# A hybrid encoder trunk on one core: quarters of the array in turn, logits of two heads in one step, and a bank shared between attention and state space

## The chip, the cores and the metric

The kernel runs on one core of a Trainium2 chip. The metric is the device time of one execution in microseconds. In the rows PE is TensorE's matmul, PEld its weight load, DVE is VectorE, ACT is ScalarE, POOL is GpSimd and SP is the queue that issues nearly all DMAs.

## The reference

Two layers work on one sequence of 256 tokens with 1024 features. All is float32.

```
h = rmsnorm(x, norm_g[l]);  proj = h @ w_in[l]            # 1024 -> 5120
xa, za, qb, kb, vb, zb, qc, kc, vc, zc = split(proj)      # ten parts of 512
ya = ssm_branch(xa, ...) * silu(za)        # 32 groups of 16 channels, 64 complex states, two directions
yb = na_branch(qb, kb, vb, rpb) * silu(zb) # 8 heads of 64, neighbourhood attention on a 4 x 64 grid
yc = dilated_branch(qc, kc, vc, t5) * silu(zc)  # 8 heads of 64, three dilated windows
x = x + concatenate([ya, yb, yc]) @ w_out[l]
```

A final rmsnorm follows. The state-space branch ends in a gated product with glu_w (512 x 512).

## The kernel before

Every step is a small Python generator. It yields the engine that it wants next, the buffer slots that it takes (`SLOTS` says how many of each there are) and the events that it waits for. A planner (`Flow`) holds a clock for each engine, adds an assumed cost for each instruction (`charge`), and always advances the step that can start first, less a patience and then by rank (`RANK`, `PATIENCE`). What comes out is one fixed order of instructions for each engine; on the chip every engine works its list off in that order.

The weights come in pieces of 512 KB (`raw`). A piece for a split product is rounded to a high part on ACT or DVE (`whi`, about 1 us) and its remainder is taken on DVE (`wlo`); then 24 matmuls use it (`mm3`, records `pj<-...`). Some pieces are used unsplit as plain float32. The step `products` runs through the pieces: 20 column blocks of w_in, then w_out and glu_w. All else stands between its matmuls in PE's list.

PSUM has eight banks, and the kernel takes all: `pj` 3, `sc` 1, `pp` 1, `po` 1, `sm` 2. The attention of a layer is 16 steps of `head` (two branches of 8 heads). A head takes `sc`, makes its logits in two matmuls with 64 rows of the array (even heads have their 64 features on partitions 0 to 63, odd ones on 64 to 127), adds the bias and takes the row maximum on DVE (tile `pt`), frees `sc`, takes exponentials on ACT, scales by the reciprocal sums, takes `pp` for four transposes, copies them to `ptt` on ACT, and after the odd head of two the products with v go to `po`. The buffers `pt`, `ptt` and `bias` have two slots each.

The state-space branch takes `sm` for all its steps. It works in 4 blocks of 8 groups, and 4 groups at a time each use 32 columns of the array (a quarter, `tile_position=(0, 32 * g4)`), so that each writes its own 32 partitions of one bank. The tiles are named after the steps: `psx` (`ssm_x`: inputs to states; it goes through the four quarters in its innermost loop already, and through whole-array transposes of the same name after that), then a scan on DVE, `psr` (`ssm_kernels`: with 16 matmuls of 128 columns and 16 of 16 columns a block), and `psy` (`ssm_y`: 24 matmuls of 128 columns a block). In `psr` and `psy` all matmuls of one quarter come before those of the next. From `psr` the kernel goes through ACT and DVE (`rs`) to DRAM and comes back as `toep`; from `psy` it goes through DRAM (`yd`) to `yT`, GELU and the gated product.

Every float32 matmul (operands not split) stands in the trace as two records.

Of the kernel before, what the change touches and what calls it, by code (L numbers as in the profile page):

```python
# [20 lines left out]
P = 128  # L21
# [4 lines left out]
HEADS = 8  # L26
HD = 64
GROUPS = 32
NST = 64
CH = 16  # L30
T = 8
# [22 lines left out]


SLOTS = dict(raw=3, whi=3, wlo=2, act=3, qkv=6, g4=8, wb=6, qrp=2, tm=3, toep=1, E=1, u=5, bias=2, t2k=2, pt=2, ptt=2,
            xa=1, sg=5, xt=1, hy=1, bd=1, bs=1, rs=1, yt=1, ys=3, tab=1, atn=1, pj=3, sc=1, pp=1, po=1, sm=2)

PLAIN = ((0, 1, 2, 3, 5, 8), (0, 1))

# [10 lines left out]
            gelu=(AF.Gelu_apprx_tanh, AF.Tanh))  # L71
# [8 lines left out]
            place=(0.4, 5.3), ssm_params=(7.3, 5.6), ssm_start_values=(7.6, 6.2), ssm_angles=1.5, normed=(2.8, 1.0),  # L80
            split_h=(0.2, 2.6), finish=(3.7, 3.1), put_out=0.7, high_parts=(4.6, 0.2), low_parts=(8.6, 8.2),
            low_by_dma=(1.5, 1.7), to_xa=(7.7, 1.9), to_u=(3.7, 8.8), to_qkv=(3.7, 5.7), to_gate=(8.0, 0.4),
            keep_x=(2.7, 8.1), head=(2.5, 0.5), gelu=(9.0, 0.2), to_mix=(5.2, 1.4), to_x=(7.4, 1.4), load_pieces=1.5,
            into_loads=(7.4, 6.4), into_powers=(0.1, 5.1), t5_rows=(1.9, 5.1), biases=(5.2, 7.9), reload_x=(1.3, 4.3),
            bias_glu=(8.7, 6.0), ssm_x=(3.8, 7.6), ssm_scan=(6.7, 3.1), ssm_kernels=(5.2, 4.9), ssm_y=(3.7, 3.6),
            ssm_tables=(2.1, 7.5), ssm_into=5.0, ssm_out=(0.8, 5.3), products=(5.2, 1.2))
# [9 lines left out]
            to_mix=(0.339, 0.3), reload_x=(-0.3, 0), bias_glu=0.1, place=(0.8, 0.195), split_h=(0.15, 0.249),  # L96
# [17 lines left out]
class Event:  # L114
    t, eng = None, None
# [24 lines left out]
def _count(x):  # L140
    n = 1
    for _, m in x.ap[1:]:
        n *= m
    return n
# [9 lines left out]
class Flow:  # L154
# [16 lines left out]
    def charge(self, eng, method, args, kw):  # L171
        out = args[0] if args else kw["out"]
        c = self.cur
        start = max(self.clock[eng], c.at, c.ready + (0.0 if c.last == eng else _latency(c.last, eng)))
        if method == "dma_start":
            spread = args[1].ap[0][1] < 64 and out.ap[0][1] == P
            self.clock[eng] = c.ready = start + (1.05 if eng == "G" else 0.65 if spread else 0.475)
            c.last = eng
            d = max(self.clock["DMA"], self.clock[eng] + 0.65)
            n = _count(out) * (out.ap[0][1] if out.ap[0][1] <= P else 1) * 4  # L180
            self.clock["DMA"] = d + max(n / 360e3, 0.06)
            c.pend = max(c.pend, self.clock["DMA"] + 0.85)
            return
        n = _count(out)
        if eng == "PE":
            if method == "transpose":
                cost = 0.109
            else:
                m, r = _count(kw["lhsT"]), kw["rhs"]
                passes = 1 if r.dtype == F32R else 4  # L190
                cost = max(_count(r) / 2400.0 * passes, 0.054) + (0.0025 if passes == 1 else 0.005)

                if m < 16:
                    pass
                elif m <= 32:
                    cost = (cost + 3 * 0.027) / 4
                elif m <= 64:
                    cost = (cost + 0.053) / 2
                else:
                    cost = max(cost, 0.107)  # L200
        elif eng == "V":
            one = method in ("tensor_scalar", "tensor_copy", "tensor_scalar_mul", "tensor_scalar_add", "memset")
            cost = 0.07 + n / (1920.0 if one else 960.0)
            if any(not isinstance(x, (float, int)) and x is not None and not isinstance(x, ALU) for x in args[2:3] if one):
                cost += 0.065
            if method == "reciprocal":
                cost = 0.06 + n * 0.0065
        elif eng == "A":
            cost = 0.1 + n * 0.00082 + (0.18 if "accum_out" in kw else 0.05 if "bias" in kw else 0.0)
            if method == "mul" and not isinstance(args[2], float):  # L210
                cost += 0.09
            if method == "activation" and args[2] in HOME and args[2] not in SETS.get(self.table, ()):
                self.table = HOME[args[2]]
                cost += 1.28
        else:
            cost = 0.1 + n * 0.0023
        if eng != "G":
            start = max(start, c.pend)
        if eng == "PE":

            if start - self.clock[eng] > IDLE:
                self.cold = start + COLD
            if start < self.cold:
                cost *= 2
        c.ready = self.clock[eng] = start + cost
        c.last = eng
# [112 lines left out]
def trunk(ctx: ExitStack, tc: tile.TileContext, io):  # L339
    nc = tc.nc  # L340
    flow = Flow(tc)
    V, A, G, PE, SP = flow.V, flow.A, flow.G, flow.PE, flow.SP
# [9 lines left out]
    def bank(tag, name=None):  # L352
        return psum.tile([P, 512], F32, name=name or tag, tag=tag, bufs=SLOTS[tag])
# [19 lines left out]
    def mm(out, lhsT, rhs, start, stop):  # L373
        PE.matmul(out, lhsT=lhsT, rhs=rhs, start=start, stop=stop, skip_group_check=True)
# [36 lines left out]
    bd = one("bd", [2, GB, CH, 2])  # L411
# [490 lines left out]
    def ssm_kernels(L, b, tb, wcs):  # L902
        bb = tb.bb
        yield "A", "bd", "bs"
        bs = new("bs", [2, GB, CH, 2])
# [4 lines left out]
        for d in range(2):  # L910
            r = slice(d * NST, (d + 1) * NST)
# [3 lines left out]
        yield "PE", "sm"  # L915
        ps = bank("sm", "psr")
        n = (T + 1) * CH
        for h in range(2):
            for g4 in range(4):
                g = 4 * h + g4  # L920
                o = ps[32 * g4:32 * g4 + 32, h * n:(h + 1) * n]
                for ri in range(2):
                    PE.matmul(o[:, :T * CH], lhsT=bd[:, ri, g].rearrange("p c d -> p (c d)"),
                              rhs=wcs[h][:, ri, g4].rearrange("p t c -> p (t c)"),
                              start=(h == 0 and ri == 0), stop=ri == 1, skip_group_check=True,
                              tile_position=(0, 32 * g4))
                for ri in range(2):
                    PE.matmul(o[:, T * CH:], lhsT=bs[:, ri, g].rearrange("p c d -> p (c d)"),
                              rhs=tb.cc[:, ri, b * GB + g], start=False, stop=ri == 1,
                              skip_group_check=True, tile_position=(0, 32 * g4))  # L930
        flow.free("bd", "bs")
        yield "A", "rs"
        rs = new("rs", [2, T + 1, CH])
# [28 lines left out]
    def ssm_y(L, b, tb):  # L962
# [8 lines left out]
        wcs, u, toep = tb.wc[b], L.u[b], tb.toep[b]  # L971
        py = bank("sm", "psy")
        for h in range(2):
            for g4 in range(4):
                g = 4 * h + g4
                o = py[32 * g4:32 * g4 + 32, h * P:(h + 1) * P]
                PE.matmul(o, lhsT=u[:, g, :], rhs=toep[:, g, :], start=h == 0, stop=False,
                          skip_group_check=True, tile_position=(0, 32 * g4))
                for ri in range(2):
                    PE.matmul(o, lhsT=hy[:, ri, g, :], rhs=wcs[h][:, ri, g4].rearrange("p t c -> p (t c)"),  # L980
                              start=False, stop=ri == 1, skip_group_check=True, tile_position=(0, 32 * g4))
        flow.free("toep" if b < TOEP else "qkv", "g4", "g4", "u", "hy")
        tb.y_left -= 1
        if tb.y_left == 0:
# [81 lines left out]
    def near(t, qt):  # L1066
        return free(t, FAR * (1 - qt), [[GRID_W, 4], [1, NEAR]])

    def grid(t, qt):
        return free(t, S * qt, [[GRID_W, 4], [1, NEAR]])  # L1070

    def head(L, br, h):
        B = L.br[br]
        hp, hh = h // 2, h % 2
        r = slice(HD * hh, HD * hh + HD)
        yield "PE", "sc", B.q_ev[hp // 2], B.k_ev[hp // 2]
        sc = bank("sc").rearrange("p (q k) -> p q k", q=2)
        for qt in range(2):
            o, q, k = sc[:, qt, :], B.qkv[0].tile[r, hp, qt * P:(qt + 1) * P], B.qkv[1].tile[r, hp, :]
            if br == 0:  # L1080
                o, k = grid(sc, qt), near(k, qt)
            mm(o, q, k, qt == 0, True)
        B.sc_left -= 1
        if B.sc_left == 0:
            flow.free("qkv", "qkv")
            if br == 1:
                flow.set(L.sc_ev)
        bias = L.bias[br]
        nm, sm = one("nm", [2], bufs=4), one("sm", [2], bufs=4)
        if br == 0:  # L1090
# [19 lines left out]
        for qt, (p, _, _) in enumerate(parts):  # L1110
            eng = yield "A/V"
            scale(eng, p, p, sm[:, qt:qt + 1])
        yield "PE", "pp"
        pp = bank("pp").rearrange("p (k q) -> p k q", k=2)
        for qt in range(2):
            for kt in range(2):
                PE.transpose(pp[:, kt, qt * P:(qt + 1) * P], pt[:, qt, kt * P:(kt + 1) * P], ident)
        flow.free("pt")

        yield ("A", "ptt", "ptt") if hh == 0 else ("A", B.ptt_ev[h - 1])  # L1120
        ptt = B.ptt[h] = new("ptt", [2, S])
        A.copy(ptt, pp)
        flow.free("pp")
        flow.set(B.ptt_ev[h])
        if hh == 0:
            return
# [266 lines left out]
    def run_layer(L):  # L1393
# [3 lines left out]
        for kind, c, kgs in L.jobs:  # L1397
            if kind == "in":
# [31 lines left out]
                if c == 1:  # L1430
                    ssm_run(L, tbs[l])
                    flow.spawn(biases(L), l)
                    for br in range(2):
                        for h in range(HEADS):
                            flow.spawn(head(L, br, h), l)
                    flow.spawn(reload_x(L), l)
                    flow.spawn(bias_glu(L), l)
            elif kind == "glu":
# [233 lines left out]
```

## Time and profile before

| what | value |
|---|---|
| median of 3 runs | 517.58 us (512.52 to 519.69) |
| the profiled execution | 511.08 us, of which 509.3 us span |
| TensorE clock granted, mean of the span | 0.981 |
| busy: PE, PEld, DVE, ACT | 95%, 86%, 75%, 58% |
| chain that ended last | PE 67%, DMA 20%, DVE 6% |

The span runs from the first to the last instruction; 1.8 us lie around it. Busy shares are means over stages that differ, so the table by stage counts for more than this one. Layer 0 takes about the first 260 us, layer 1 the rest.

### The profile page before, as it was taken

What the parts mean: (1) busy time and instruction counts of PE and PEld (TensorE: products, weight loads), DVE (VectorE), ACT (ScalarE), POOL (GpSimd) and SP (SyncE); (2) the same over time, 40 slices, a digit from 0 to 9 for tenths busy, and PEclk for the clock granted to TensorE, in tenths of its full rate; (3) what the DMA queues carried; (4) which work ended last, traced back from release to release, by engine and by line L of the source; (5) the groups of instructions that cost most, each with busy time, mean ns of one, the idle gap of its engine ahead of it and who ended that gap; (6) DMA issues with size and microseconds to landing.
All of it is one profiled execution on the core that took longest, in us unless ns stands there. A gap on an engine that the chain in (4) does not pass through costs nothing.

```text
span 509.3 us, 10599 instructions
## 1 busy us (share of the span) xinstructions
PE 483.6 (95%) x4076; PEld 436.0 (86%) x4076; DVE 381.3 (75%) x745; ACT 297.0 (58%) x596; POOL 24.6 (5%) x45
## 2 busy tenths in 40 slices
PE   8887988999999999989999699999999999999995
PEld 7676786698888999989998599998989799999995
DVE  5966767988997895457879678889788994358533
ACT  6432366566587665455545436767676776587432
POOL 1000102110000000000000010222000000000000
PEclk9988999999999999999999889999999999999999
DMA  7987798865663779874767997877565585664512
GB/s 261 299 236 247 218 258 232 222 172 166 140 143 106 219 260 278 245 215 162 252 205 211 262 268 204 186 170 178 136 126 134 138 261 182 184 167 168 187 41 84
DMA packets 73331, 99.61 MB, mean 196 GB/s; under 512 B 26768, under 2 KB 48400, under 8 KB 73280
## 3 DMA queue, kind: packets, MB, share of 16 engines
q1 hardware_dynamic: 73136, 98.83, 70.1%
q8 instruction: 32, 0.52, 0.4%
q14 instruction: 19, 0.16, 0.1%
q10 hardware_dynamic: 144, 0.10, 0.1%
HBM read 93.19 MB, written 5.72 MB: 194 GB/s over the span
## 4 chain that ended last, share of the span: by engine, by line
PE 67%; DMA 20%; DVE 6%; SPq 2%; ACT 2%; issue 2%; POOL 0%; DVEq 0%; POOLq 0%; ACTq 0%
PE pj L135 45%; PE psr L135 6%; PE sc L135 5%; DMA raw<-w_in 4%; DMA wb<-b_c 3%; DMA u<-xad 3%; PE po L135 3%; PE pp L135 3%; PE psy L135 3%; SPq L135 2%; DVE wb L135 2%; PE psx L135 2%; DMA qd<-qbt 2%; DMA raw<-w_out 1%; DMA xad<-xa 1%
## 5 line engine op out<-in xcount | busy, mean ns | idle before, releaser
L135 DVE TENSOR_TENSOR wlo<-raw,whi 128x1024 fp32r<-128x1024 f32 x92 | 113.6, 1234 | 55.6 <-PE pj L135 28.6
L135 ACT CAST whi<-raw 128x1024 fp32r<-128x1024 f32 x91 | 95.0, 1048 | 67.3 <-DMA raw<-w_in 28.2
L135 PE MATMUL pj<-h0h,whi 128*128 128x256 f32 x192 | 58.3, 304 | 0.0
L135 PE MATMUL pj<-h1h,whi 128*128 128x256 f32 x192 | 56.3, 293 | 0.0
L135 PE MATMUL pj<-h0h,wlo 128*128 128x256 f32 x192 | 55.1, 287 | 0.7 <-DVE wlo L135 0.7
L135 PE MATMUL pj<-h0l,whi 128*128 128x256 f32 x192 | 54.9, 286 | 0.0
L135 PE MATMUL pj<-h1h,wlo 128*128 128x256 f32 x192 | 53.9, 281 | 0.0
L135 PE MATMUL pj<-h1l,whi 128*128 128x256 f32 x192 | 53.9, 281 | 0.0
L135 PEld LDWEIGHTS pj<-h0h,whi 128*128 128x128 f32 x192 | 37.4, 195 | 5.7 <-issue 5.5
L135 PEld LDWEIGHTS pj<-h1h,whi 128*128 128x128 f32 x192 | 36.3, 189 | 2.7 <-issue 2.7
L135 PEld LDWEIGHTS pj<-h0h,wlo 128*128 128x128 f32 x192 | 37.3, 194 | 1.0 <-DVE wlo L135 0.9
L135 PEld LDWEIGHTS pj<-h0l,whi 128*128 128x128 f32 x192 | 37.3, 194 | 0.0
L135 PEld LDWEIGHTS pj<-h1h,wlo 128*128 128x128 f32 x192 | 36.2, 189 | 0.0
L135 PEld LDWEIGHTS pj<-h1l,whi 128*128 128x128 f32 x192 | 36.1, 188 | 0.0
L135 PE MATMUL pj<-xin,raw 128*128 128x256 f32 x128 | 32.5, 404 | 3.6 <-DMA raw<-w_in 2.8
L135 ACT ACTIVATE pt<-pt,sm 128x160 f32<-128x160 f32 (+1 forms) x63 | 28.3, 469 | 10.5 <-DVE sm L135 10.2
L135 PEld LDWEIGHTS pj<-xin,raw 128*128 128x128 f32 x128 | 24.5, 200 | 10.2 <-DVE xin L135 3.0
L135 PE MATMUL sc<-k,q 64*128 64x256 f32 (+1 forms) x128 | 31.0, 362 | 2.1 <-DVE nm L135 2.1
L135 ACT ACTIVATE pt<-pt,nm 128x160 f32<-128x160 f32 (+1 forms) x64 | 29.8, 468 | 5.3 <-DVE nm L135 5.1
L135 PE MATMUL psr<-wc,bd 128*32 128x128 f32 x256 | 31.1, 279 | 0.0
L135 POOL TENSOR_TENSOR bias<-bias,namask 128x320 f32<-128x320 f32 x16 | 19.5, 1220 | 222.8 <-DMA bias<-rpb 99.9
L135 PEld LDWEIGHTS sc<-k,q 64*128 64x128 f32 x128 | 19.8, 186 | 9.9 <-DVE nm L135 3.6
(198 smaller groups left out, 1300.5 us busy)
## 6 DMA issues: line engine op xcount, KB each, us to landing
raw<-w_in SPq DMA_DIRECT2D x78, 512.0 KB, 4.6
raw<-w_out SPq DMA_DIRECT2D x24, 512.0 KB, 3.4
wb<-b_c SPq DMA_DIRECT2D x32, 256.0 KB, 7.7
qrp<-qd SPq DMA_DIRECT2D x32, 256.0 KB, 5.0
bias<-vdram SPq DMA_DIRECT2D x16, 256.0 KB, 4.9
toep<-rd SPq DMA_DIRECT2D x64, 64.0 KB, 3.9
bias<-rpb SPq DMA_DIRECT2D x32, 116.0 KB, 5.5
raw<-glu_w SPq DMA_DIRECT2D x4, 512.0 KB, 4.0
```

Source lines behind the costliest of these rows:

```text
L135: return f(*args, **kw)
```

## The change

Four things are changed.

- In `ssm_kernels` and `ssm_y` the loop over the four quarters becomes the innermost one: the same matmuls on the same operands, in another order.
- A new step `pair` takes two `sc` banks and makes the logits of two heads, alternating between the even head (rows 0 to 63) and the odd one (rows 64 to 127). It then spawns two `head` steps that go on as before, each with its bank. `sc` gets 2 banks.
- `pp` has no bank of its own any more: the transposes of the probabilities take one of the two `sm` banks. The even head of two takes its `ptt` slots before its transposes and no longer after them; the odd one waits before its transposes for the even one's copy.
- The planner's cost of a matmul with 64 rows is about halved, and `pair` has the rank that `head` had.

```
-            xa=1, sg=5, xt=1, hy=1, bd=1, bs=1, rs=1, yt=1, ys=3, tab=1, atn=1, pj=3, sc=1, pp=1, po=1, sm=2)
+            xa=1, sg=5, xt=1, hy=1, bd=1, bs=1, rs=1, yt=1, ys=3, tab=1, atn=1, pj=3, sc=2, po=1, sm=2)
...
+                elif rows == 64:
+                    cost = (cost + 0.053) / 2
...
         for h in range(2):
-            for g4 in range(4):
-                g = 4 * h + g4
-                o = ps[32 * g4:32 * g4 + 32, h * n:(h + 1) * n]
-                for ri in range(2):
-                    PE.matmul(o[:, :T * CH], lhsT=bd[:, ri, g].rearrange("p c d -> p (c d)"),
+            for ri in range(2):
+                for g4 in range(4):
+                    PE.matmul(ps[32 * g4:32 * g4 + 32, h * n:h * n + T * CH],
+                              lhsT=bd[:, ri, 4 * h + g4].rearrange("p c d -> p (c d)"),
...
-                for ri in range(2):
-                    PE.matmul(o[:, T * CH:], lhsT=bs[:, ri, g].rearrange("p c d -> p (c d)"),
+            for ri in range(2):
+                for g4 in range(4):
+                    g = 4 * h + g4
+                    PE.matmul(ps[32 * g4:32 * g4 + 32, h * n + T * CH:(h + 1) * n],
...
-            for g4 in range(4):
-                g = 4 * h + g4
-                o = py[32 * g4:32 * g4 + 32, h * P:(h + 1) * P]
-                PE.matmul(o, lhsT=u[:, g, :], rhs=toep[:, g, :], start=h == 0, stop=False,
+            for part in range(3):
+                for g4 in range(4):
+                    g = 4 * h + g4
+                    PE.matmul(py[32 * g4:32 * g4 + 32, h * P:(h + 1) * P],
+                              lhsT=u[:, g, :] if part == 0 else hy[:, part - 1, g, :],
...
-    def head(L, br, h):
+    def pair(L, br, hp):
+
         B = L.br[br]
-        yield "PE", "sc", B.q_ev[hp // 2], B.k_ev[hp // 2]
-        sc = bank("sc").rearrange("p (q k) -> p q k", q=2)
+        yield "PE", "sc", "sc", B.q_ev[hp // 2], B.k_ev[hp // 2]
+        scs = [bank("sc").rearrange("p (q k) -> p q k", q=2) for _ in range(2)]
         for qt in range(2):
-            o, q, k = sc[:, qt, :], B.qkv[0].tile[r, hp, qt * P:(qt + 1) * P], B.qkv[1].tile[r, hp, :]
-            if br == 0:
-                o, k = grid(sc, qt), near(k, qt)
-            mm(o, q, k, qt == 0, True)
-        B.sc_left -= 1
+            for hh in range(2):
+                r = slice(HD * hh, HD * hh + HD)
+                o, q, k = scs[hh][:, qt, :], B.qkv[0].tile[r, hp, qt * P:(qt + 1) * P], B.qkv[1].tile[r, hp, :]
+                if br == 0:
+                    o, k = grid(scs[hh], qt), near(k, qt)
+                mm(o, q, k, qt == 0, True)
+        B.sc_left -= 2
...
+        for hh in range(2):
+            flow.spawn(head(L, br, 2 * hp + hh, scs[hh]), L.l)
+
+    def head(L, br, h, sc):
...
-        yield "PE", "pp"
-        pp = bank("pp").rearrange("p (k q) -> p k q", k=2)
+
+        yield ("PE", "sm", "ptt", "ptt") if hh == 0 else ("PE", "sm", B.ptt_ev[h - 1])
+        pp = bank("sm", "pp").rearrange("p (k q) -> p k q", k=2)
...
-        yield ("A", "ptt", "ptt") if hh == 0 else ("A", B.ptt_ev[h - 1])
+        yield "A"
         ptt = B.ptt[h] = new("ptt", [2, S])
         A.copy(ptt, pp)
-        flow.free("pp")
+        flow.free("sm")
```

## Rows read from the trace of the kernel before

**Rows 1.** The page: busy time by engine, and the chain by line.
```profile
PE 483.6 (95%) x4076; PEld 436.0 (86%) x4076; DVE 381.3 (75%) x745; ACT 297.0 (58%) x596; POOL 24.6 (5%) x45
...
PE pj L135 45%; PE psr L135 6%; PE sc L135 5%; DMA raw<-w_in 4%; DMA wb<-b_c 3%; DMA u<-xad 3%; PE po L135 3%; PE pp L135 3%; PE psy L135 3%; SPq L135 2%; DVE wb L135 2%; PE psx L135 2%; DMA qd<-qbt 2%; DMA raw<-w_out 1%; DMA xad<-xa 1%
```

**Rows 2.** Windows by stage: length, busy PE, PEld, DVE, ACT, POOL, granted clock, DMA share, GB/s.
```profile
55.00:100.00 45.00, 40.99 (x281) 31.62 (x279) 36.20 (x74) 25.80 (x60) 8.76 (x13) 1.00 0.86 233
100.00:180.00 80.00, 80.00 (x741) 70.59 (x741) 70.90 (x146) 55.24 (x129) 1.53 (x4) 1.00 0.59 155
180.00:230.00 50.00, 47.38 (x487) 45.37 (x487) 30.33 (x51) 26.76 (x41) 0.22 (x1) 0.97 0.87 253
...
300.00:420.00 120.00, 120.00 (x1062) 106.90 (x1060) 107.25 (x213) 83.57 (x190) 9.49 (x12) 1.00 0.71 174
420.00:446.00 26.00, 26.00 (x319) 24.10 (x318) 9.63 (x11) 14.93 (x26) 0.00 (x0) 1.00 0.65 183
```

**Rows 3.** The chain that ended last, in order of time: start, duration, what.
```profile
105.14 3.93 PE psr L135 x57
...
125.11 1.06 PE sc L135 x4
...
192.26 6.85 DMA toep<-rd
...
307.51 0.74 PE sc L135 x4
...
423.46 2.51 PE psy L135 x48
```

**Rows 4.** Timeline of PE in one block of `psr`: start, duration, instruction.
```profile
105.07 0.62 PE L135 MATMUL psr<-wc,bd 128*32 128x128 f32 x4
105.53 0.18 PE L135 MATMUL psr<-cc,bs 128*32 128x16 f32 x1
105.53 0.30 PE L135 MATMUL psr<-wc,bd 128*32 128x128 f32 x1
105.56 0.25 PE L135 MATMUL psr<-cc,bs 128*32 128x16 f32 x3
...
106.00 0.30 PE L135 MATMUL psr<-wc,bd 128*32 128x128 f32 x1
```

**Rows 5.** Timeline of PE in two bursts of `psx` (quarters in turn) and what follows each.
```profile
58.00 0.64 PE L135 MATMUL psx<-wb,u 128*32 128x256 f32 x8 [0.30 <-DMA u<-xad]
58.57 0.70 PE L135 MATMUL pj<-xin,raw 128*128 128x256 f32 x2
...
77.35 1.07 PE L135 MATMUL psx<-wb,u 128*32 128x256 f32 x16
78.35 0.39 PE L135 MATMUL pj<-whi,h0h 128*128 128x256 f32 x1
```

**Rows 6.** `sc` alone by the windows of rows 2: length, busy PE, PEld, DVE.
```profile
100.00:180.00 80.00, 9.83 (x36) 5.91 (x36) 7.29 (x18) 1.00 0.59 155
...
300.00:420.00 120.00, 15.48 (x64) 9.88 (x64) 11.82 (x32) 1.00 0.71 174
```

**Rows 7.** Waits of the whole span: who for whom, us in total, times, longest.
```profile
DVE wlo L135 <- PE pj L135: 28.6, 16, 4.6
...
ACT rs L135 <- PE psr L135: 20.9, 8, 3.9
...
DVE rs L135 <- ACT rs L135: 11.2, 7, 2.0
```

**Rows 8.** ACT's groups in 100 to 180 us: count, busy us, mean ns.
```profile
L135 ACT ACTIVATE pt<-pt,nm 128x256 f32<-128x256 f32 (+1 forms) x20 | 9.8, 492 | 0.0
L135 ACT ACTIVATE pt<-pt,sm 128x256 f32<-128x256 f32 (+1 forms) x20 | 9.6, 494 | 4.3 <-DVE sm L135 4.3
L135 ACT COPY ptt<-pp 128x512 f32<-128x512 f32 x11 | 6.4, 586 | 1.6 <-PE pp L135 1.6
```

**Rows 9.** DVE's group of the logits in the same stretch.
```profile
L135 DVE CUSTOM_DVE_ANT_0 pt<-sc,bias 128x256 f32<-128x256 f32 x16 | 6.7, 417 | 1.2 <-ACT ptt L135 0.9 <-issue 0.2
```

More of the change, by code (lines that the diff above doesn't have):

```diff
@@ L82 @@
             low_by_dma=(1.5, 1.7), to_xa=(7.7, 1.9), to_u=(3.7, 8.8), to_qkv=(3.7, 5.7), to_gate=(8.0, 0.4),
-            keep_x=(2.7, 8.1), head=(2.5, 0.5), gelu=(9.0, 0.2), to_mix=(5.2, 1.4), to_x=(7.4, 1.4), load_pieces=1.5,
+            keep_x=(2.7, 8.1), pair=(2.5, 0.5), head=(2.5, 0.5), gelu=(9.0, 0.2), to_mix=(5.2, 1.4), to_x=(7.4, 1.4), load_pieces=1.5,
             into_loads=(7.4, 6.4), into_powers=(0.1, 5.1), t5_rows=(1.9, 5.1), biases=(5.2, 7.9), reload_x=(1.3, 4.3),
@@ L188, in charge @@
             else:
-                m, r = _count(kw["lhsT"]), kw["rhs"]
+                m, r, rows = _count(kw["lhsT"]), kw["rhs"], kw["lhsT"].ap[0][1]
                 passes = 1 if r.dtype == F32R else 4
@@ L926, in ssm_kernels @@
                               tile_position=(0, 32 * g4))
-                for ri in range(2):
-                    PE.matmul(o[:, T * CH:], lhsT=bs[:, ri, g].rearrange("p c d -> p (c d)"),
+            for ri in range(2):
+                for g4 in range(4):
+                    g = 4 * h + g4
+                    PE.matmul(ps[32 * g4:32 * g4 + 32, h * n + T * CH:(h + 1) * n],
+                              lhsT=bs[:, ri, g].rearrange("p c d -> p (c d)"),
                               rhs=tb.cc[:, ri, b * GB + g], start=False, stop=ri == 1,
@@ L973, in ssm_y @@
         for h in range(2):
-            for g4 in range(4):
-                g = 4 * h + g4
-                o = py[32 * g4:32 * g4 + 32, h * P:(h + 1) * P]
-                PE.matmul(o, lhsT=u[:, g, :], rhs=toep[:, g, :], start=h == 0, stop=False,
[L978 to L981, printed above, removed]
+            for part in range(3):
[3 more added lines that the diff above has]
+                              lhsT=u[:, g, :] if part == 0 else hy[:, part - 1, g, :],
+                              rhs=toep[:, g, :] if part == 0 else wcs[h][:, part - 1, g4].rearrange("p t c -> p (t c)"),
+                              start=h == 0 and part == 0, stop=part == 2, skip_group_check=True,
+                              tile_position=(0, 32 * g4))
         flow.free("toep" if b < TOEP else "qkv", "g4", "g4", "u", "hy")
@@ L1070, in grid @@
         return free(t, S * qt, [[GRID_W, 4], [1, NEAR]])
-    def head(L, br, h):
+    def pair(L, br, hp):
         B = L.br[br]
-        hp, hh = h // 2, h % 2
-        r = slice(HD * hh, HD * hh + HD)
-        yield "PE", "sc", B.q_ev[hp // 2], B.k_ev[hp // 2]
-        sc = bank("sc").rearrange("p (q k) -> p q k", q=2)
+        yield "PE", "sc", "sc", B.q_ev[hp // 2], B.k_ev[hp // 2]
+        scs = [bank("sc").rearrange("p (q k) -> p q k", q=2) for _ in range(2)]
         for qt in range(2):
-            o, q, k = sc[:, qt, :], B.qkv[0].tile[r, hp, qt * P:(qt + 1) * P], B.qkv[1].tile[r, hp, :]
-            if br == 0:
-                o, k = grid(sc, qt), near(k, qt)
-            mm(o, q, k, qt == 0, True)
-        B.sc_left -= 1
+            for hh in range(2):
[5 more added lines that the diff above has]
+        B.sc_left -= 2
         if B.sc_left == 0:
@@ L1087, in head @@
                 flow.set(L.sc_ev)
+        for hh in range(2):
+            flow.spawn(head(L, br, 2 * hp + hh, scs[hh]), L.l)
+    def head(L, br, h, sc):
+        B = L.br[br]
+        hp, hh = h // 2, h % 2
         bias = L.bias[br]
@@ L1433, in run_layer @@
                     for br in range(2):
-                        for h in range(HEADS):
-                            flow.spawn(head(L, br, h), l)
+                        for hp in range(HEADS // 2):
+                            flow.spawn(pair(L, br, hp), l)
                     flow.spawn(reload_x(L), l)
```

## The prediction, made before the changed kernel ran

> **What bounds the kernel now.** I read four views, from coarse to fine. The page comes first: PE is busy 95% of the span, and the chain that ended last passes through `psr` for 6%, `sc` for 5% and `psy` for 3% of it [rows 1]. These are the three sets of matmuls that the change reorders, so nearly all of their time is on the path today. Second, the windows by stage: the reader is to see that PE has no idle time in 100 to 180, 300 to 420 and 420 to 446 us, but that DVE is close behind in the first two, 70.9 of 80 us and 107.25 of 120, and far behind in the third, 9.63 of 26. In 180 to 230 the DMA share is 0.87, and in 55 to 100 PE is idle for 4.0 of 45 us [rows 2]. Third, the chain in order of time says which burst costs what, and that in 180 to 230 the end is set by transfers such as the 6.85 us of `toep`, not by PE [rows 3]. Fourth, the timelines of PE say how the matmuls of a burst lie against one another [rows 4, 5].
>
> **Quarters in turn, `psr`.** A block takes 3.93 us on PE [rows 3], and in it the next quarter begins 0.47 us after the one before (105.53 to 106.00) [rows 4]; eight such steps and the edges make the 3.93. So a quarter runs nearly alone, with its four records of 128 columns one after another. `psx` already has the order that the change gives to `psr`: 8 records of 256 columns take 0.57 us to the next matmul, 16 take 1.00 [rows 5]. The 8 more cost 0.43 us, so four quarters run at once, each with one record per 0.215 us, and 0.14 us are a fixed cost of the burst. A record of 128 columns then costs a quarter 0.108 us. The records of 16 columns follow one another in 0.03 us (three of 0.18 us within 0.25) [rows 4]. In the new order a quarter has 8 records of 128 and 8 of 16 columns in a block: 0.14 + 8 x 0.108 + 8 x 0.03 = 1.25 us. That takes 2.68 us off each block, 10.7 a layer, 21.4 in all. The other bound: the densest burst with mixed operands is `psy`, 48 records in 2.51 us [rows 3], 0.049 each without the fixed cost. At that rate `psr` would take 3.3 us and save 0.65 a block, 5 in all. I take 1.25, since `psx` is the row with the same order.
>
> **Quarters in turn, `psy`.** A block has 48 records of 128 columns, 12 a quarter: 0.14 + 12 x 0.108 = 1.44 us in place of 2.51, 1.07 less, 4.3 a layer (at the other bound nothing).
>
> **A rule against it.** The page "TensorE: Matmul & The Clock Gate" of the Trainium skill, Part 3, The mechanism, says that a weight load overlaps matmuls in flight only where it goes to other rows of the array. The quarters all use 128 rows, so by that rule they would gain nothing, and only the logits would. The trace speaks against it: 8 records of `psx` one after another would take 8 x 0.215 = 1.72 us, and took 0.57 [rows 5].
>
> **Logits of two heads.** A head's burst takes 0.74 us in the first branch, where a record has 160 columns, and 1.06 in the second, with 256 [rows 3]. The 4 x 96 columns between them cost 0.32, so a record costs 0.139 or 0.222 and the burst 0.18 besides. No row shows two halves of the rows at work together. If they run together, a pair takes what one head took, and 8 x 0.74 + 8 x 1.06 = 14.4 us go. If they run one after another, only one fixed cost a pair goes, 16 x 0.18 = 2.9. I take 14.4, since the nearest row, `psx`, shows parts of the array with own banks or partitions running together. By stage, half of the busy time of `sc` is 4.9 us in 100 to 180 and 7.7 in 300 to 420 [rows 6].
>
> **The shared bank and the new waits.** The transposes lose their own bank; they share two with `psx`, `psr` and `psy`. A bank is held until ACT has copied it, 0.586 us for `ptt` [rows 8]. The even head's transposes now stand behind its `ptt` slots, so behind the products with v of the pair before; what is queued behind them on PE are the product matmuls, and ACT's copy waits for them. The planner puts other product matmuls first, which is the cover; I cost it at nothing. If the cover is gone, each of the 32 transposes costs up to one copy, 32 x 0.586 = 18.8 us. Against that, `psr` holds its bank 2.68 us less. A pair gives DVE four maxima of 0.417 us in a row [rows 9] in place of two, and holds the bank meanwhile; nothing else takes `sc` in that time. The planner's cheaper price for logits only moves orders; I cost that between -6 and +6 us (the longest single wait of DVE for a product, 4.6 us, is of this size [rows 7]) and take zero. No step is moved past SP or POOL, and no DMA is added.
>
> **The sum.** PE loses 10.7 + 4.9 = 15.6 of 80 us in 100 to 180, and 10.7 + 7.7 = 18.4 of 120 in 300 to 420. But then DVE is late next. Its 70.9 and 107.25 busy us are a floor; its idle time there is 9.1 and 12.75 us [rows 2]. Of the idle time 11.2 us, some 5.6 a layer, is its wait for ACT's copy of `psr`, which itself waits for PE [rows 7]; that part goes with the faster `psr`. So the first stage gets shorter by 5.6 to 9.1 us and the second by 5.6 to 12.75; I take the middles, 7.4 and 9.2. In 420 to 446 DVE and ACT have room, and the four blocks of `psy` give their full 4.3. In 180 to 230 transfers set the end, and in 55 to 100 PE waits anyway: nothing there, at most 4.3 and 2.8. The sum is 7.4 + 9.2 + 4.3 = 20.9, say 21 us off the profiled execution's 511.08, which makes 490. That execution is the fastest of the four that are shown; their mean (511.08, 512.52, 517.58, 519.69) is 515.2, and the median of the three timed ones is 517.58. I take the mean less 21: 494. About 2% is what a measurement of this kernel can tell from no change, some 10 us.
>
> **The rivals.**
> - **All of it comes through.** DVE's remainders `wlo` may slide into stages where it has room (it is busy 30 of 50 us after 180 and 10 of 26 after 420 [rows 2]), so that PE keeps setting the pace: 15.6 + 18.4 + 4.3, and 4.3 + 2.8 from the other stages, make 45, and the time 470. For it: DVE waits 28.6 us for products to give a buffer back [rows 7]. Against it: two `wlo` slots let it run only two pieces ahead. Chance 0.12.
> - **The shared bank gives it back.** Transposes wait for a copy on ACT in nearly every head: 21 - 18.8 leaves 2, so 513. For it: ACT is at 55 of 80 us and its copies come late (the copy of `psr` waited 20.9 us in 8 times [rows 7]); against it: the filler of products. Chance 0.16.
> - **Two row halves don't run together.** A pair then saves only one fixed cost of 0.18 us: in 100 to 180 (4.5 pairs) PE needs 80 - 10.7 - 0.8 = 68.5 us, still under DVE's floor, and in 300 to 420 (8 pairs) about 108, near it. The price is some 1 to 3 us: 496. This is the case in which the change doesn't do what it says, and it ends near the forecast. Chance 0.10.
> - **The quarters don't run together,** as that rule of the skill has it. By the rows, `psr` and `psy` stay, the logits give 4.9 + 7.7, less what DVE holds back: some 11, so 504. Chance 0.03.
> - **Attention becomes the long pole, and it is slower.** A pair is one chain: logits 1.06, four maxima of 0.42, four exponentials of 0.49, four scalings of 0.49, two bursts of transposes of 0.59, two copies of 0.59, products with v of about 1: some 10 us without any wait [rows 3, 8, 9]. Now only one even head at a time may have transposes, until the pair's products with v are done. A layer's 8 pairs have some 112 us at present (logits from 307.5 on [rows 3], all 16 heads before 420 [rows 6]), 14 a pair. If waits behind a long DVE or ACT instruction stretch a pair to more than 14 us, and pairs don't overlap, attention sets the stage. At 17 us a layer's stage is 24 us longer; with two layers and the gains of `psy` left (about 9) that is 515 + 48 - 9 less the waits that PE fills, and I put it at 530. Against it: a pair's logits, maxima and exponentials can still overlap the pair before, as `sc` and `pt` come free earlier. Chance 0.07.
>
> **How the numbers follow.** The forecast has 0.52, the rivals 0.12, 0.16, 0.10, 0.03 and 0.07. The forecast's own range is 484 to 504: the stage bounds (5.6 + 5.6 + 4.3 to 9.1 + 12.75 + 4.3), moved by part of the order's 6 us. For 8 in 10, the range leaves out the slower case, the far half of the first rival and part of the shared bank's: 477 to 511. Faster by over 2% (under 505) are the forecast, the first, the third and most of the fourth rival, and a small part of the shared bank's: 0.79. Within 2%: 0.15. Slower: 0.06.
>
> **What would show it.** In the changed kernel's profile a `psr` block stands at about 1.25 us on PE, a `psy` block at 1.44, and a burst of 8 `sc` records at 0.74 or 1.06. PE's share falls and DVE's share in the stages of the heads goes over 95%, with PE waiting for `wlo`; the waits of ACT and DVE for `psr` shrink to a third. Should PE idle for long, its clock could drop; in 55 to 100, at 41 of 45 us busy, it kept 1.00 [rows 2], so I expect no more drops than now. Wrong would be: `psr` still near 4 us, transposes waiting for `sm` or `ptt` copies, or a stage whose last wait is for a head's products with v.

## The result, and the profile after

The changed kernel takes 494.58 us (median of 4 runs, 489.38 to 495.53), the kernel before 515.64 in the same comparison (512.52 to 519.69): a ratio of 0.957, with an interval of 0.947 to 0.967. 21.1 us went, where 21 were forecast. The profiled executions have spans of 492.0 and 509.3 us, 17.3 apart; all that is counted by stage below is counted in these two. The profiled execution of before (511.08 us) lies below all four timed ones, so 17.3 is the smaller of the two differences.

First the bursts themselves. Timeline of PE after, in a block of `psr`: start, duration, instruction.

```profile
103.61 0.64 PE L135 MATMUL psr<-wc,bd 128*32 128x128 f32 x16
104.07 0.29 PE L135 MATMUL psr<-cc,bs 128*32 128x16 f32 x16
104.19 0.62 PE L135 MATMUL psr<-wc,bd 128*32 128x128 f32 x16
104.63 0.29 PE L135 MATMUL psr<-cc,bs 128*32 128x16 f32 x16
104.86 0.39 PE L135 MATMUL pj<-h0h,whi 128*128 128x256 f32 x1
```

From the first record to the next product 1.25 us pass, where the chain of before had 3.93 [rows 3]; there a quarter's records were set down one after another [rows 4], here 16 records of all four quarters make one entry of 0.64. Now a block of `psy` and a pair of heads in the second branch, in the same timeline.

```profile
354.52 1.13 PE L135 MATMUL sc<-k,q 64*128 64x256 f32 x8
355.58 0.66 PE L135 MATMUL pp<-ident,pt 128*128 128x128 f32 x4
...
405.10 0.43 PE L135 MATMUL psy<-toep,u 128*32 128x128 f32 x8
405.35 0.62 PE L135 MATMUL psy<-wc,hy 128*32 128x128 f32 x16
405.78 0.40 PE L135 MATMUL psy<-toep,u 128*32 128x128 f32 x8
406.00 0.62 PE L135 MATMUL psy<-wc,hy 128*32 128x128 f32 x16
406.55 0.39 PE L135 MATMUL pj<-h1h,whi 128*128 128x256 f32 x1
```

`psy` takes 1.45 us (2.51 before), and the 8 records of two heads 1.06, as long as the 4 of one head did [rows 3]. So each of the three bursts can have the length that was worked out for it. All eight blocks of `psr` have it and seven of the eight of `psy` (the first of layer 0 stops for 1.29 us inside, waiting for ACT's `hy`). Of the 16 pairs only ten have it; the other six take 1.03 to 2.05 us. One of those six:

```profile
368.31 0.70 PE L135 MATMUL sc<-k,q 64*128 64x256 f32 x2
369.20 1.13 PE L135 MATMUL sc<-k,q 64*128 64x256 f32 x6 [0.19 <-DVE nm L135]
```

From 368.31 to the next product at 370.26 these are 1.95 us, not 1.06. After the first matmul PE stops until DVE has taken the maxima of an earlier head and with that frees the pair's second bank. `sc` keeps PE busy for 18.9 us in all, where it was 31.0 before: 12.0 went. PE's row on the page after:

```profile
PE 458.4 (93%) x4156; PEld 412.5 (84%) x4156; DVE 376.9 (77%) x742; ACT 297.0 (60%) x599; POOL 22.9 (5%) x45
```

Among the matmuls are `warm`, filler that computes nothing: 7.79 us before, 19.53 after. Without it PE is busy 475.8 us before and 438.9 after: 36.9 us of matmul time are gone. The time in which PE does nothing useful grew from 33.5 to 53.1 us. So 19.6 of the 36.9 came back as idle time, and 17.3 came off the span.

Where, the next two views show: windows of the whole program between landmarks (first logits of layer 0, its first `psy`, its last state-space gate, then the same three of layer 1, and the end). The columns are as in [rows 2]. Before:

```profile
55.83:185.82 129.99, 125.98 (x1066) 107.45 (x1065) 112.27 (x225) 83.69 (x193) 10.30 (x17) 1.00 0.69 189
185.82:237.00 51.18, 48.56 (x494) 46.68 (x494) 29.58 (x52) 26.51 (x42) 0.22 (x1) 0.97 0.83 239
237.00:307.44 70.44, 65.68 (x497) 60.73 (x496) 56.64 (x86) 34.70 (x61) 2.25 (x4) 0.95 0.82 234
307.44:423.39 115.95, 115.95 (x1022) 102.82 (x1021) 103.76 (x207) 83.31 (x189) 9.49 (x12) 1.00 0.69 168
423.39:466.85 43.46, 43.46 (x470) 42.27 (x470) 21.01 (x25) 28.26 (x41) 0.00 (x0) 1.00 0.62 181
466.85:509.29 42.44, 37.14 (x315) 36.57 (x313) 21.02 (x33) 17.94 (x30) 0.00 (x0) 0.97 0.32 105
```

After:

```profile
56.42:186.26 129.84, 123.48 (x1180) 106.00 (x1179) 116.91 (x229) 87.18 (x197) 9.49 (x17) 1.00 0.77 212
186.26:232.31 46.05, 39.61 (x458) 37.68 (x458) 25.09 (x47) 26.02 (x47) 0.22 (x1) 0.96 0.77 211
232.31:303.50 71.19, 66.65 (x500) 61.36 (x498) 56.93 (x86) 33.72 (x57) 2.13 (x4) 0.95 0.81 225
303.50:405.10 101.60, 99.89 (x1026) 88.60 (x1026) 98.08 (x205) 82.29 (x189) 8.00 (x12) 1.00 0.74 190
405.10:445.67 40.57, 39.18 (x464) 37.47 (x464) 21.14 (x26) 27.34 (x41) 0.00 (x0) 1.00 0.67 192
445.67:492.02 46.35, 41.20 (x315) 40.89 (x313) 21.04 (x33) 17.91 (x30) 0.00 (x0) 0.84 0.31 97
```

The stages change by -0.2, -5.1, +0.8, -14.4, -2.9 and +3.9 us, and 0.6 come ahead of the first landmark. Three things are to be seen.

**The heads of layer 0 are not shorter, but hold more.** The count of matmuls in the first stage goes up from 1066 to 1180 though a pair has as many as two heads (18 of the 114 are filler). The planner's order put 816 records of products ahead of the first `psy`, where it had 720; 96 of them at 0.119 us are 11.4 us of work moved ahead, and with it pieces `wlo` on DVE (28 where there were 23).

**What was moved ahead is missing afterwards.** `warm` alone in the first two windows of after:

```profile
56.42:186.26 129.84, 2.10 (x18) 2.09 (x18) 1.00 0.77 212
186.26:232.31 46.05, 6.49 (x57) 6.33 (x56) 0.96 0.77 211
```

In the second stage PE has 46.05 - 39.61 + 6.49 = 12.9 us without useful work, before it had 2.6 of 51.18. The timeline of all engines after says what it waits for (SPq is SP's queue; the bracket is the idle time ahead and who ended it):

```profile
213.07 6.42 PE L438 MATMUL warm<-ident 128*128 128x128 f32 x56
...
217.25 0.37 SPq L135 DMA_DIRECT2D yT<-yd  x1
...
222.80 1.12 ACT L135 CAST g2h<-yT 128x512 fp32r<-128x512 f32 x2
...
223.97 0.38 PE L135 MATMUL pj<-g2h,whi 128*128 128x256 f32 x1 [4.48 <-ACT g2h L135]
```

The last `psy` of the layer was done at 205.7. Its result then goes to DRAM, comes back as `yT`, goes through GELU and is split. From 213.07 to 223.97 PE has no piece left whose other operand is there: 6.42 us of filler and 4.48 of waiting. The transfers are not all of this way. SP issues the last store `yd` only at 210.62 us, behind loads of `wb`, and ahead of the GELU ACT waits 4.57 us for a piece of w_out that stands earlier in its list.

**The end got longer at half the clock.** The last window has the same 315 matmuls and a granted clock of 0.84 in place of 0.97. What this costs has its own experiments below.

Of the waits, ACT's for `psr` (20.9 us [rows 7]) is 0.6 us, and DVE's behind it (11.2) is no longer on the list. DVE's wait for products to give back a buffer is 19.4 us, from 28.6 [rows 7].

### The profile page after: what moved, and what is told of

It is laid out like the page before. It is cut to its first block, busy times and chain, and to the rows that moved or that the text cites. A ratio compares the mean times of both kernels' runs of the same rounds, so it can differ in the third digit from the quotient of the medians.

```text
span 492.0 us, 10772 instructions
## 1 busy us (share of the span) xinstructions
PE 458.4 (93%) x4156; PEld 412.5 (84%) x4156; DVE 376.9 (77%) x742; ACT 297.0 (60%) x599; POOL 22.9 (5%) x45
## 5 line engine op out<-in xcount | busy, mean ns | idle before, releaser
L135 DVE TENSOR_TENSOR wlo<-raw,whi 128x1024 fp32r<-128x1024 f32 x92 | 113.5, 1234 | 41.2 <-PE pj L135 19.4
L135 ACT CAST whi<-raw 128x1024 fp32r<-128x1024 f32 x92 | 96.0, 1046 | 77.0 <-DMA raw<-w_in 38.6
L135 POOL TENSOR_TENSOR bias<-bias,namask 128x320 f32<-128x320 f32 x16 | 17.8, 1112 | 223.2 <-DMA bias<-rpb 209.5
L135 DVE TENSOR_TENSOR wb<-wb,qrp 128x1024 f32<-128x1024 f32 x16 | 20.2, 1261 | 6.6 <-DMA qrp<-qd 6.5
L135 DVE TENSOR_TENSOR wc<-cc,qsd 128x512 f32<-128x512 f32 x32 | 23.1, 726 | 0.0
L135 ACT COPY ptt<-pp 128x512 f32<-128x512 f32 x32 | 18.6, 581 | 5.7 <-PE pp L135 5.5
```

The costliest lines, as they stand in the source:

```text
L135: return f(*args, **kw)
```

## The experiments

The theory after the result: the quarters give nearly all, the pairs free time of PE that DVE then withholds. The rivals: the pairs give as much; the planner's new order, not DVE, is what eats the rest.

**The quarters alone.** The kernel before with the two loop changes in `psr` and `psy`; the rest of every engine's order stays as it was.

```
-            for g4 in range(4):
-                g = 4 * h + g4
...
-                for ri in range(2):
+            for ri in range(2):
+                for g4 in range(4):
...
-            for g4 in range(4):
+            for part in range(3):
+                for g4 in range(4):
```

> The kernel before with the quarters in turn in psr and psy alone; the order of every other instruction is that of before. Theory A (freed time of PE counts, up to what DVE allows in the stages of the heads): psr goes to 1.25 us and psy to 1.45, 30 us less on PE; the first psy of layer 0 hardly moves, since DVE sets that stage, the one of layer 1 comes some 8 us earlier, and the whole is 14 to 18 us shorter (about 499). Theory B (the gain comes from the new order that the pairs bring, and faster psr and psy only turn into waits for DVE): less than 6 us, above 509.

Measured: 495.52 us, ratio 0.962 (0.954 to 0.971). Its windows between the landmarks, heads of layer 0, heads of layer 1, and the end:

```profile
54.45:177.80 123.35, 117.47 (x1065) 98.04 (x1064) 110.34 (x224) 82.76 (x193) 9.59 (x17) 0.99 0.74 200
...
297.46:405.24 107.78, 105.21 (x1022) 91.94 (x1021) 101.12 (x207) 83.41 (x189) 8.52 (x12) 1.00 0.72 179
...
444.43:488.95 44.52, 39.62 (x315) 39.31 (x313) 21.04 (x33) 17.94 (x30) 0.00 (x0) 0.87 0.32 102
```

At the same order, the heads of layer 0 lose 6.6 us and those of layer 1 8.2; PE's busy time loses 8.5 and 10.7 there, and PE is now idle for 5.9 and 2.6 us. The four `psy` blocks of layer 1 give 4.3 (43.46 to 39.19). The last stage, untouched by the edit, is 2.1 longer, at a clock of 0.87. The quarters alone nearly have the whole result. That is more than the 14 to 18 us that were expected, and it was not expected that the first `psy` of layer 0 would move: it comes 8.0 us sooner (177.80, from 185.82).

**The pairs, with the bank and the price.** The changed kernel with the old loop order in `psr` and `psy`; all else, the order included, is that of the changed kernel.

```
-            for ri in range(2):
-                for g4 in range(4):
+            for g4 in range(4):
+                g = 4 * h + g4
...
+                for ri in range(2):
```

> The changed kernel with psr and psy put back to one quarter after the other; order of every other instruction as in the changed kernel. Theory A: sc gives 12 to 14 us of PE, DVE holds back about half of it and ACT and DVE still wait for psr at 3.9 us a block; 4 to 9 us shorter than before (507 to 511). Theory B: most of the 21 us remain, below 500.

Measured: 511.27, ratio 0.994 (0.989 to 0.998). The groups of its page:

```profile
L135 PE MATMUL psr<-wc,bd 128*32 128x128 f32 x256 | 31.1, 279 | 0.0
...
L135 PE MATMUL sc<-k,q 64*128 64x256 f32 (+1 forms) x128 | 16.8, 364 | 0.8 <-DVE nm L135 0.8
```

`sc` has 16.8 us of busy time (31.0 before), so 14.2 are gone, and 3 to 4 us reach the time, just under the 4 to 9 that were expected. Beside the quarters the pairs bring 0.962 to 0.957, which is inside the intervals.

**Row halves without alternation.** The changed kernel with the two heads' logits one after the other.

```
-        for qt in range(2):
-            for hh in range(2):
+        for hh in range(2):
+            for qt in range(2):
```

> The changed kernel, but the pair makes both matmuls of the even head and then both of the odd one, in place of alternating; all else in the same order. If matmuls on other rows start as soon as they are at the head of the list, whatever stands before them in their own half, the burst of 8 records stays at about 0.74 and 1.06 us and the time is that of the changed kernel (494). If the halves overlap only when they alternate, the burst grows to 1.3 and 2.0 us, PE loses 11 us again and the time is 2 to 6 us longer.

Measured: 492.49, ratio 0.957 (0.946 to 0.967), the same as with alternation. A pair of the first branch in its timeline:

```profile
53.72 0.82 PE L135 MATMUL sc<-k,q 64*128 64x160 f32 x8
54.47 0.48 PE L135 MATMUL pj<-xin,raw 128*128 128x256 f32 x1
```

0.75 us for 8 records, 0.74 with alternation. The halves run beside each other even if all four records of one come first. What shortens the logits is that two heads stand in one step; the order within it shows no effect.

**The shared bank alone.** The kernel before, its transposes in `sm`, with the waits for `ptt` that go with that; one bank lies unused. The planner's order changes with it.

```
-  ... pj=3, sc=1, pp=1, po=1, sm=2)
+  ... pj=3, sc=1, po=1, sm=2)
...
-        yield "PE", "pp"
-        pp = bank("pp").rearrange("p (k q) -> p k q", k=2)
+        yield ("PE", "sm", "ptt", "ptt") if hh == 0 else ("PE", "sm", B.ptt_ev[h - 1])
+        pp = bank("sm", "pp").rearrange("p (k q) -> p k q", k=2)
...
-        flow.free("pp")
+        flow.free("sm")
```

> The kernel before with the transposed probabilities in the two sm banks and the new waits for ptt ahead of the transposes, and nothing else of the change; one PSUM bank stays unused. Theory A: the waits are covered by product matmuls, within 5 us of before (511 to 521). The rival of the shared bank: each of 32 transposes waits for a copy of 0.59 us, up to 19 us longer (525 to 535).

Measured: 518.5, ratio 1.010 (1.005 to 1.015): a loss of 5 us. In it the first `psy` of layer 1 has 2080 records of products ahead of it, where the kernel before has 1960. A wait for a copy in each head would have been up to 18.8 us. PE's list of waits has none of the transposes for a copy; its longest entry is for `u` (6.1 us, 4.4 before). So the bank's price isn't such a wait; that it is the different order is likely but not shown.

**Less work for DVE.** The scan's cross product, one multiplication and one addition of each step on DVE, is left out, so the states aren't those of the reference; the planner is charged for both as before, so that the order stays. Once in the changed kernel, once in the kernel before.

```
-            V.tensor_mul(a2, swapped(E, src, RS, dims), lamsw(n, bc))
+            flow.charge("V", "tensor_mul", (a2,), {})
...
-            V.tensor_add(a1, a1, a2)
+            flow.charge("V", "tensor_add", (a1,), {})
```

> The changed kernel with the cross product of the scan left out: its multiplication into t2s and the addition of it (so the states lack their imaginary coupling), some 13 us of DVE in each layer's stage of the heads; the planner still counts both, so the order stays. Theory A (in the changed kernel DVE sets the stages of the heads): both stages get shorter by 6 to 10 us, 12 to 18 in all (477 to 483). Rival (PE or the order sets them): below 6 us.

> The kernel before with the same work of the scan left out. Theory A: PE has no idle time in the stages of the heads there, so the same 26 us of DVE are worth little, 2 to 7 us (508 to 513), clearly less than in the changed kernel. Rival: as much as there.

Measured: 485.32 in the changed kernel, ratio 0.944 (0.936 to 0.952), where the changed kernel has 0.957: 9.3 us below its median, with intervals that overlap a little, and 7.4 in the spans (492.0 and 484.6). In the kernel before 513.16, ratio 1.000 (0.997 to 1.003). The heads of layer 1 without the cross product, in the changed kernel:

```profile
300.77:399.99 99.22, 98.00 (x1028) 87.81 (x1027) 88.64 (x182) 82.38 (x189) 8.93 (x12) 1.00 0.76 199
```

and in the kernel before:

```profile
309.00:425.28 116.28, 115.71 (x1021) 102.61 (x1020) 92.33 (x184) 83.00 (x189) 7.92 (x12) 1.00 0.69 173
```

Before, 11.4 us less of DVE (103.76 to 92.33) do nothing, since PE is busy all the time: it was the bound there. After, 9.4 us less of DVE (98.08 to 88.64) make the stage 2.4 us shorter, and PE fills up to 98.00 of 99.22. So DVE does bind the heads of layer 1 after the change, but with little behind it: PE is again next, only some 2 us away. Where it binds can be read from `sc` alone in that stage, in the changed kernel and without the cross product:

```profile
303.50:405.10 101.60, 9.64 (x64) 5.89 (x64) 11.48 (x32) 1.00 0.74 190
300.77:399.99 99.22, 8.26 (x64) 5.32 (x64) 11.17 (x32) 1.00 0.76 199
```

1.4 of the 2.4 us are bursts of logits: the two last pairs, which took 1.95 and 1.88 us, take 1.06 when DVE frees their second bank sooner. The heads of layer 0 without the cross product, in the changed kernel:

```profile
56.33:186.91 130.58, 123.47 (x1180) 106.50 (x1179) 108.62 (x208) 88.12 (x198) 9.24 (x17) 0.99 0.77 212
```

Here 8.3 us less of DVE (116.91 to 108.62) make the stage no shorter (129.84 to 130.58), so DVE doesn't bind it. What else came off the span came off outside the heads, and no run here says why. Neither theory's number was met: 12 to 18 would have been DVE as the sole bound, under 6 no bound.

**One product on POOL.** The products `tmo` of the scan go from DVE to GpSimd, in the changed kernel.

```
-                yield "V", "g4", "tm", tb.ev, tb.wb_ev[2 * NB - 1]
+                yield "G", "g4", "tm", tb.ev, tb.wb_ev[2 * NB - 1]
...
-                V.tensor_mul(tm, cbc(tb.csum, 0), qbc(tb.qc, 0))
+                G.tensor_mul(tm, cbc(tb.csum, 0), qbc(tb.qc, 0))
```

> The changed kernel with one product of ssm_out (tmo, 0.69 us on DVE, 16 of them, 11 us) done on POOL, which is 5% busy. Theory A: a faster version, 4 to 8 us under the changed kernel (486 to 490), if the new order does no harm; if POOL's longer instruction (about 2 us) or its wait for a bias in its list holds the products up, no gain (493 to 500).

Measured: 501.42, ratio 0.970 (0.961 to 0.979): no gain. It is 6.8 us above the changed kernel, with intervals that overlap a little. Its group:

```profile
L135 POOL TENSOR_TENSOR tmo<-csum,qc 128x512 f32<-128x512 f32 x16 | 26.0, 1623 | 78.7 <-DVE wc L135 35.7 <-DVE sm L135 27.4 <-DVE t1s L135 9.5
```

1.62 us for each, where DVE takes 0.71 in the changed kernel, and a new order besides. It doesn't tell the two apart.

**The old price for logits.** The changed kernel, with the planner's cost of a matmul with 64 rows as before. The instructions are the same, only their order is another.

```
-                elif rows == 64:
-                    cost = (cost + 0.053) / 2
```

> The changed kernel without the planner's lower price for matmuls with 64 rows, so that only the plan differs (another order of nearly all instructions after the first heads). If the price matters little beside the matmuls themselves, within 5 us of the changed kernel (490 to 500). If the gain hangs on the plan that this price makes, 505 or more.

Measured: 507.27, ratio 0.989 (0.982 to 0.996): 12.7 us above the changed kernel by the medians, and some 16 by the two ratios, as the two were timed in separate comparisons. This is the second case, 505 or more. The `psr` blocks still take 1.25 us. The first `psy` of layer 1 stands at 427.0 us behind 2080 records of products (405.1 behind 1966 in the changed kernel), and a wait that is 1.3 us in the changed kernel has grown (who for whom, us, times, longest):

```profile
PE psy L135 <- ACT hy L135: 7.2, 2, 6.7
```

The 6.7 us stand in layer 0, at 200 to 207 us, and the granted clock is 0.52 in the 9 us that follow. The order that the price makes is worth more than the pairs.

**The quarters of `psr` only.** The kernel before with the first of the two loop changes.

```
-            for g4 in range(4):
-                g = 4 * h + g4
...
-                for ri in range(2):
+            for ri in range(2):
+                for g4 in range(4):
```

> The kernel before with the quarters in turn in psr alone: 21.4 of the 30 us that both take off PE. Theory A: 70% of the 20 us that both gave, 12 to 15 us (500 to 503); the stages of the heads gain as with both (first psy of layer 0 about 8 us sooner), and the 4 us a layer of psy are missing after it. Rival (psr only moves the wait to DVE, and it was psy that gave the time): under 7 us.

Measured: 498.58, ratio 0.974 (0.966 to 0.982). By the ratios 13.3 us of a total of 19.4 are from `psr`, as expected; `psy` brings about 6, though the two intervals overlap (0.954 to 0.971 for both).

**The end in whole columns.** Last, the longer end. Windows of 5 us near the end of the changed kernel:

```profile
472.00:477.00 5.00, 5.00 (x47) 5.00 (x46) 1.00 (x2) 1.54 (x3) 0.00 (x0) 1.00 0.00 0
477.00:482.00 5.00, 5.00 (x26) 5.00 (x26) 0.76 (x5) 1.37 (x4) 0.00 (x0) 0.51 0.00 0
482.00:487.00 5.00, 4.87 (x23) 4.57 (x22) 2.45 (x8) 1.37 (x4) 0.00 (x0) 0.50 0.36 105
```

The clock falls from 2.4 to 1.2 GHz at 477 us, with PE busy in all of the 5 us before and after. The timeline there:

```profile
476.94 0.27 PE L135 MATMUL pj<-mix2h,wlo 128*128 128x128 f32 x1
477.05 0.32 PE L135 MATMUL pj<-mix2l,whi 128*128 128x128 f32 x1
477.16 0.42 PE L135 MATMUL pj<-mix2h,whi 128*128 128x128 f32 x1
477.38 0.42 PE L135 MATMUL pj<-mix2h,wlo 128*128 128x128 f32 x1
```

Their distance goes from 0.11 to 0.22 us. These are matmuls of 128 columns, since the last column block is made in two halves of 128 tokens. In the experiment it is made in two halves of its features, with all 256 tokens in each, so with half as many matmuls, each of 256 columns: in the changed kernel, in the kernel before, and in the one with the quarters alone.

```
-  parts = [((i,), slice(0, S)) for i in range(2)] if l < DEPTH - 1 else
-          [((0, 1), slice(i * P, (i + 1) * P)) for i in range(2)]
+  parts = [((i,), slice(0, S)) for i in range(2)]
...
-        yield ("A",) + tuple(L.out_ev[:4 + t])
+        yield ("A",) + tuple(L.out_ev)
```

> The changed kernel with the last column block of the last layer in two halves of output features with 256 tokens each, in place of two halves of tokens with 128. If the clock of TensorE falls at 477 us because of the matmuls of 128 columns before it, it now stays at 1.00 until PE is nearly done, and the end comes 1 to 4 us sooner (490 to 493), less what the two halves of tokens gained by overlap. If it falls for another reason, the time is the same or 1 to 2 us longer.

> The kernel before with the same edit of the last column block alone. Its clock stays up until PE is done anyway, so what is left is half of the 48 matmuls at 0.118 us, 2.8 us, less the overlap of the two halves of tokens: 0 to 3 us faster (512 to 515). If the whole 6 us that the edit gave to the changed kernel come from fewer matmuls, 509.

> Quarters in turn alone, with the last column block of the last layer in two halves of features with 256 tokens each. By e1 (495.5, clock down from 477.6 us on) and the 6 us that the same edit gave to the changed kernel: 488 to 491, and the clock at 1.00 until PE is nearly done. If the pairs are worth something once the clock stays up, this is 2 to 5 us above the changed kernel with the same edit (488.8); if not, level with it.

Measured: 488.78 in the changed kernel, ratio 0.952 (0.946 to 0.958), below its 490 to 493; 509.9 in the kernel before, 0.995 (0.990 to 0.999); 493.03 with the quarters alone, 0.958 (0.949 to 0.967), above its 488 to 491. The same windows in the changed kernel with whole columns:

```profile
472.00:477.00 5.00, 5.00 (x46) 5.00 (x45) 1.12 (x2) 2.25 (x5) 0.00 (x0) 1.00 0.00 0
477.00:482.00 5.00, 3.49 (x25) 2.73 (x23) 3.29 (x12) 1.34 (x4) 0.00 (x0) 1.00 0.00 1
```

The clock stays at 1.00. From the last gate to the end it is 41.55, 41.38 and 41.5 us in the three, where it was 46.35, 42.44 and 44.52 with halves of tokens. In the profiled execution of before the clock didn't fall until PE was done:

```profile
494.00:499.00 5.00, 5.00 (x47) 5.00 (x46) 1.12 (x2) 2.19 (x5) 0.00 (x0) 1.00 0.01 3
499.00:504.00 5.00, 4.84 (x40) 4.42 (x39) 2.99 (x11) 2.08 (x7) 0.00 (x0) 1.00 0.16 46
```

There the edit is worth 1.1 us. So in the profiled executions the fall of the clock costs the changed kernel about 3.9 us and the quarters alone about 2.1.

The timed executions don't bear out that the kernel before is spared. By the medians the edit is worth 5.1 us there (515.02 to 509.9, nearly the 509 of the second case), by the ratio 2.6. In the same comparison the mean clock of the 13 executions without the edit goes from 0.965 to 0.985, and of the ten with it nine have 0.979 or more and lie within 508.1 to 512.2 us. So it is likely that the clock falls in some executions of the kernel before too; only one was profiled, so this isn't shown. The profiles of the other kernels here with halves of tokens have the fall too, also the one with the pairs and the old loop order (0.50 in 493 to 498 us), except for the two made from the kernel before without the loop changes (the shared bank, and less work for DVE).

The changed kernel with whole columns has the lowest median of all kernels here that compute everything. It is clear of the kernel before, but not of the changed one, whose interval overlaps.

## Why the prediction was right, and where it was not

- **The quarters, `psr` and `psy`.** 1.25 and 1.44 us were worked out, 1.25 and 1.45 measured. Taking `psx` as the row with the same order was right, and the other bound, the rate of the old `psy`, was that of the old order. The rule of the Trainium skill ("TensorE: Matmul & The Clock Gate", Part 3, The mechanism), that a weight load overlaps matmuls in flight only on other rows, doesn't hold in these runs: the quarters all use 128 rows and went from 3.93 to 1.25. That quarters gain nothing by it was my inference.
- **The logits.** That the row halves run together was right: 0.74 and 1.06 for a pair were forecast, and ten of 16 pairs measure it. But "nothing else takes `sc` in that time" was wrong, as the next pair does. Six pairs stop inside their burst until DVE frees the second bank, and `sc` gives 12.0 us in place of 14.4.
- **The cap.** The busy time of `psr`, `psy` and `sc` fell by 42 us (32.0 to 10.6, 24.0 to 15.4, 31.0 to 18.9). 36.9 of useful matmul time went, as other matmuls took 5 longer: `pj` 4.3 of them, with 1.9 in the last stage at its lower clock. 17.3 came off the span. That the rest would be held back was right, and the rival in which all of it comes through was wrong. But the sign that I named, PE waiting for `wlo`, did not come: it is 0.8 us in layer 0's heads and nothing in layer 1's.
- **The sum by stage.** At an unchanged order (quarters alone, for which the cap gives the same terms) 7.4, 9.2 and 4.3 measured 6.6, 8.2 and 4.3. In the changed kernel they did not stand where I put them: 0.2 in layer 0's heads, 14.4 in layer 1's, which is beyond the 12.75 that DVE's floor was to leave, and 5.1 in 180 to 230, where I expected nothing. DVE's floor was worked out from a fixed stretch, but its work slides: 5.7 us of it left the stage of layer 1, and 4.6 came into that of layer 0. The total was right with errors of 4 to 7 us a stage that partly cancel, so how near it came, 21.1 for 21, is luck.
- **What is late next.** I named DVE for the heads of both layers. In layer 1 it is (96.5% busy), by 2.4 us and mostly through the second `sc` bank; PE, filled up by the planner, is right behind. In layer 0 it isn't: DVE is 90% busy there, and 8.3 us less of its work made the stage no shorter. What layer 0 lacks comes after its heads, on `psy`'s way through SP's list, DRAM and ACT to the gated product, with 10.9 us of filler and waiting. In that stretch the prediction had only the transfers into `psy`.
- **The planner's price, -6 to +6, taken as zero.** This term was mis-sized: the new price is worth 12.7 us or more in its kernel. I had taken one wait of DVE as the size of an order, when an order sets all of them.
- **The shared bank, taken as zero.** Alone it costs 5 us. The forecast of a wait for a copy in every head didn't come true. The even head's wait for `ptt`, the new limit on pairs, didn't make attention the long pole: the stage of layer 1 is shorter, not longer.
- **The clock.** I expected no more drops than before, because I looked for idle time of PE. In the profiled execution the drop came without any, and cost 3.9 us. How much of the 21.1 it takes isn't shown, since the kernel before may drop too.

**What stays open.** How much the pairs themselves give: pairs, bank and price each come with an order of their own (-4, +5, and 12.7 for the price), and no run holds the order while it changes one of them. And what decides whether the clock falls in the last stage: with the quarters alone the same matmuls stand in the same order there as before, and it fell in one profiled execution and not in the other. It may differ from one execution of the same kernel to the next.

## What to carry to other kernels

Where several matmuls use different columns of the array, put them in turn, since order alone took a burst from 3.93 to 1.25 us. Count time that is freed on the busiest engine only up to what is late next, and look for that in each stage, a path through DRAM included. A step that takes two buffers at once waits for the later of them: ask who holds the second. Where a planner writes the order, a change that moves its order carries an unknown of about 2% of the time, so try the edit alone at the old order first.

## What the hardware showed that I had not expected

- The granted clock went from 1.00 to 0.51 while PE was busy 5.00 of 5 us and had no idle time in the 5 us before. It did so in eight of the eleven profiled executions with halves of tokens (the last stage takes 46.35 us in the changed kernel and 44.52 with the quarters alone), not in that of the kernel before, which has the same matmuls there (42.44), and in none of the three with whole columns (41.4 to 41.6).
- Two halves of the rows overlap without alternation (0.75 us for 8 records, 0.74 with it), whereas quarters of the columns one after another take 0.47 us each in `psr` [rows 4].
